# Three edits to the order of the loads: weight sums one pair later, early activations behind the last weights with two more raw buffers, fetches from the fourth block on

## The chip, the core and the metric

The kernel runs on one core of one Trainium2 chip. The metric is the device time in microseconds of one execution. Before the change it is 1907.91 us, the median of three runs (1906.57 to 1908.58). PE is TensorE, DVE is VectorE, ACT is ScalarE, POOL is GpSimd, and SP is SyncE, which here only issues DMAs.

## The reference, cut to what matters

One decoder layer on 512 tokens of width 2048, in float32: sliding-window attention with sinks, then a gated MLP with a causal convolution of width 3 over the positions.

```python
h = rms_norm(x, norm_g[i, 0])
m = swa_sink_attention(h, swa_w_in[j], swa_w_out[j], swa_sinks[j], rel_bias_table)
x = x + rms_norm(m, norm_g[i, 1])
h = rms_norm(x, norm_g[i, 2])
...
u = h @ w_up                                  # 2048 x 11264
c = conv_w[0] * up[:, 0:S] + ...              # three positions
gate, val = jnp.split(c, 2, axis=-1)          # 5632 columns each
x = x + rms_norm((silu(gate) * val) @ w_down, norm_g[i, 3])   # 5632 x 2048
```

The change touches only the MLP: the end of the preparation for its up-projection `h @ w_up`, and the passage from there to the down-projection `... @ w_down`.

## The kernel before, in words

**Numbers.** Each float32 operand is split into a high and a low half: ACT writes the high half, DVE subtracts it for the low half (`split`, L63 to L65). A product is three matmuls (`prod`, L88): high by high and the two mixed ones. The halves of weights live in a ring of slots (`halves`), five of them (`wsp`) in the up-projection, each 4 KB and 4 KB per partition, and eight in the down-projection, where the other three (`wsp3`) lie where the normalized activations `ah`, `al` were.

**Up-projection.** The 5632 gate columns and 5632 value columns are cut into 44 pairs of blocks of 128 columns, `f` = 0 to 43. Pairs 0 to 3 are multiplied in the plain way, pair 3 by halves of the tokens (`up_by_tokens`), because the operands `forms[7]` and `forms[1]` are written over parts of `ah` and `al` as soon as these have been used: their sources wait in the tiles k7 and k1 (pool `tk`). Pairs 4 to 43 use Strassen's scheme in Winograd's form (`up_pair`, L691): four weight blocks of 512 KB (`bw`, six buffers), four sums of them on DVE, seven half-size products of 24 matmuls of 256 columns each, that is 168 matmuls per pair. Then `gate` (L588) does the convolution, the SiLU and the multiplication on ACT and DVE, and POOL issues the store of the result to the DRAM tensor `hd`.

**Sums of down-projection weights.** The down-projection uses the same scheme on 22 blocks (`kp`). Four sums of weights for each are made ahead of time and stored in the DRAM tensor `td`. Those of kp 0 to 5 are made before; those of kp 6 to 21 beside the up-projection, in two ways: `weight_sums` (four loads issued by SP, four additions on DVE, four stores issued by POOL) and `queue_sums` (four loads on SP, additions and stores as DMAs of POOL). Both use the four buffers `ts` of pool `tsu`, which lies on the right side of the on-chip memory, where k7 and k1 were. In the loop over pairs (`i = f - 4`) `weight_sums` starts ahead of each pair with `i % 5 == 0`, its additions lie in the pair after it, and `queue_sums` follows that pair.

**Passage to the down-projection.** After `kp` has reached 22 (in the round `i` = 36, that is pair 40) pool `tsu` is closed and a tile of 16 KB per partition is opened in its place for blocks 0 to 15 of the activations `hd[1, 0]`; four fetches of 512 KB for it are put into SP's queue there (L741, L742). The rest of that quarter (`hq10b`, blocks 16 to 21) and the other three quarters are fetched within the first three products of the down-projection, one fetch at every second weight block (L799). These tiles, and the second pair of buffers for raw weights (`wraw2`), lie in space that pools of the up-projection held: the forms, the convolution's tiles `c`, the weight blocks.

**Down-projection.** Seven products (`product`, L793), each over 22 blocks; each block is one weight load of 512 KB (`weight_form`, L781, from `td` or from the weights themselves), a split, and 12 matmuls of 512 columns. Every four blocks `act_form` makes the halves of the activations. Raw weights have four buffers: `wraw` and `wraw2`, two each, used in turn.

**What sets the order.** Matmuls (`mm`) and the SP loads that go through `in_turn` (L138) are pinned to the order of the program on their engine, so SP issues the loads, `ts`, `bw`, fetches and raw weights strictly one after another, and one that has to wait holds all behind it. The order on ACT, DVE and POOL is laid out by the planner when the kernel is built (`schedule_with_timeline_sim=True`); on the chip each engine follows its list in order.

Of the kernel before, what the change touches and what calls it, by code (L numbers as in the profile page):

```python
# [11 lines left out]
F32 = mybir.dt.float32  # L12
# [6 lines left out]
P = 128  # L19
# [16 lines left out]
NP = NF // 2  # L36
HALF = S // 2
# [4 lines left out]
def trunk(ctx, tc, xT, x, grow, table, onehot, masked, sinks, conv,  # L42
          wkv, wq, wo, wup, wdn, out):
    nc = tc.nc
    pool = lambda name, bufs, **kw: tc.tile_pool(name=name, bufs=bufs, **kw)

    const = ctx.enter_context(pool("const", 1))
    wraw = ctx.enter_context(pool("wraw", 2))
# [8 lines left out]
    def bank(i):  # L57
        return ps.tile([P, 512], F32, name=f"b{i}", bufs=1)
# [4 lines left out]
    def split(hi, lo, src):  # L63
        nc.scalar.activation(hi, src, AF.Copy)  # L64
        nc.vector.tensor_tensor(lo, src, hi.bitcast(F32), ALU.subtract)  # L65

    def halves():
        p = ring["slots"][ring["next"] % len(ring["slots"])]
        ring["next"] += 1
        return p.tile([P, 1024], F32R, name="wh"), p.tile([P, 1024], F32R, name="wl")  # L70
# [67 lines left out]
    def in_turn(o, i):  # L138
        tc.keep_in_program_order(nc.sync.dma_start(o, i))  # L139

    def weight_sums(kp, sums, paced=False):
        t = [sums.tile([P, 1024], F32, name="ts") for _ in range(4)]
        for q in (0, 2, 1, 3):
            (in_turn if paced else nc.gpsimd.dma_start)(t[q], wdn[4 * kp + q])
        yield
        for q, o in ((2, 0), (0, 1), (1, 2), (3, 1)):
            nc.vector.tensor_tensor(t[q], t[q], t[o], ALU.add)
            nc.gpsimd.dma_start(td[kp, :, q, :], t[q])
            yield

    def queue_sums(kp, sums):
        t = [sums.tile([P, 1024], F32, name="ts") for _ in range(4)]
        for q in (2, 0, 1, 3):
            in_turn(t[q], wdn[4 * kp + q])

        def add(q, o):
            nc.gpsimd.dma_start(t[q], o, accum_op=ALU.add)

        def store(q):
            nc.gpsimd.dma_start(td[kp, :, q, :], t[q])  # L160

        add(2, wdn[4 * kp])
        add(0, wdn[4 * kp + 1])
        store(2)
        add(1, t[2])
        store(0)
        add(3, t[1])
        store(1)
        store(3)

    def step(g, n=1):
        for _ in range(n):
            next(g, None)

    with ExitStack() as att:
# [10 lines left out]
        with ExitStack() as ph:  # L186
# [26 lines left out]
            for kt in range(KT):  # L213
                if kt == 0:
                    for h in range(2):
# [3 lines left out]
                        if h == 0:  # L219
                            w = halves()  # L220
                            raw = wraw.tile([P, 1024], F32, name="raw")
# [241 lines left out]
    with ExitStack() as op:  # L463
        sums = op.enter_context(pool("tso", 4))
# [5 lines left out]
        g1 = gp.tile([P, D], F32, name="g1")  # L470
# [63 lines left out]
        for b, bk in enumerate((2, 5, 6, 7)):  # L534
            o = bank(bk)
            for kt in range(KT):
# [3 lines left out]
                if b < 2:  # L540
                    if kt == 0:
                        g = weight_sums(4 + b, sums)
# [23 lines left out]
    batches = [(g, min(g + GB, NP)) for g in range(0, NP, GB)]  # L566
    hq = {}

    def fetch(m, par, g0, g1):
        t, k0 = next((t, k) for t, k, k1 in hq[m, par] if k <= g0 < k1)  # L570
        in_turn(t[:, g0 - k0:g1 - k0, :], hd[m, par, :, g0:g1, :])

    with ExitStack() as us:
# [14 lines left out]
        def gate(f, o):  # L588
            cg = conv_half(o[0], f, 0)
            nc.scalar.activation(cg, cg, AF.Silu)  # L590
            cv = conv_half(o[1], f, 1)
            nc.vector.tensor_tensor(cv, cg, cv, ALU.mult)  # L592
            kp, par = divmod(f, 2)
            nc.gpsimd.dma_start(hd[:, par, :, kp, :].rearrange("m p t -> p m t"),  # L594
                              cv.rearrange("p (m t) -> p m t", m=2))
# [71 lines left out]
        tsu = ExitStack()  # L667
        sums = tsu.enter_context(pool("tsu", 4, side="right"))

        def block(f, r, c):  # L670
            t = bw.tile([P, 1024], F32, name="bw")
            in_turn(t, wup[4 * f + 2 * c + r])
            return t

        def form(t):
            w = halves()
            split(*w, t)
            return w

        def times(o, n, w, fresh):  # L680
            o3 = o[:, :HALF].rearrange("p (a b) -> p a b", a=2)
            a = forms[n]
            for k in range(8):
                prod(o3, cols(w, k), tuple(v[:, :, k, :] for v in a), fresh and k == 0, k == 7, not fresh)

        def shot(o, name):
            t = un.tile([P, HALF], F32, name=name)
            nc.scalar.activation(t, o[:, :HALF], AF.Copy)  # L688
            return t

        def up_pair(f, g):  # L691
            X, Y, Z = (bank(k) for k in ((0, 1, 6), (3, 4, 7))[f % 2])
            ug = un.tile([P, S], F32, name="ug", bufs=2)
            uv = un.tile([P, S], F32, name="uv", bufs=2)
            b11, b21 = block(f, 0, 0), block(f, 1, 0)
            t = wraw.tile([P, 1024], F32, name="raw")
            nc.vector.tensor_tensor(t, b11, b21, ALU.add)  # L697
            times(X, 2, form(t), True)
            s1 = shot(X, "s1")
            step(g)  # L700
            b12 = block(f, 0, 1)
            times(Z, 7, form(b12), True)
            s7 = shot(Z, "s7")
            nc.vector.tensor_tensor(t, t, b12, ALU.add)
            times(X, 5, form(t), False)
            s2 = shot(X, "s2")
            step(g)
            nc.vector.tensor_tensor(b11, b11, b12, ALU.add)  # L708
            times(Z, 6, form(b11), False)
            b22 = block(f, 1, 1)  # L710
            nc.vector.tensor_tensor(t, t, b22, ALU.add)
            times(X, 3, form(t), False)
            s3 = shot(X, "s3")
            step(g)
            nc.vector.tensor_tensor(ug[:, :HALF], Z[:, :HALF], s2, ALU.subtract)
            times(Y, 1, form(b21), True)
            nc.vector.tensor_tensor(uv[:, :HALF], s3, s7, ALU.subtract)
            times(X, 4, form(b22), False)
            nc.vector.tensor_tensor(ug[:, HALF:], s1, Y[:, :HALF], ALU.subtract)
            nc.scalar.activation(uv[:, HALF:], X[:, :HALF], AF.Copy, scale=-1.0)  # L720
            gate(f, (ug, uv))

        kp = 6
        for f in range(4, NF):
            i = f - 4
            if i % 5 == 0 and kp < NP:
                work = weight_sums(kp, sums, True)
                step(work)
                kp += 1
            up_pair(f, work if i % 5 == 1 else iter(()))  # L730
            if i % 5 == 1:
                step(work)
            if i % 5 == 1 and kp < NP:
                queue_sums(kp, sums)
                kp += 1
            if kp == NP and tsu:
                tsu.close()
                tsu = None
                early = ctx.enter_context(pool("early", 1, side="right"))
                hq[1, 0] = [(early.tile([P, 16, HALF], F32, name="hq10"), 0, 16)]  # L740
                for g0, g1 in batches[:4]:  # L741
                    fetch(1, 0, g0, g1)  # L742


    acts.close()
# [3 lines left out]
    y = acc.tile([P, NT, D], F32, name="y")  # L749
    g3 = acc.tile([P, D], F32, name="g3")  # L750
    rest = ctx.enter_context(pool("rest", 1))
    hq[1, 0].append((rest.tile([P, NP - 16, HALF], F32, name="hq10b"), 16, NP))
    raws = (wraw, ctx.enter_context(pool("wraw2", 2)))
    for m, par in ((0, 1), (1, 1)):
        hq[m, par] = [(rest.tile([P, NP, HALF], F32, name=f"hq{m}{par}"), 0, NP)]
    small = ctx.enter_context(pool("small3", 4))
    last = ctx.enter_context(ExitStack())
    hq[0, 0] = [(last.enter_context(pool("hq00", 1)).tile([P, NP, HALF], F32, name="hq00"), 0, NP)]
    coming = [(1, 0, *g) for g in batches[4:]] + [(*q, *g) for q in ((0, 0), (0, 1), (1, 1)) for g in batches]
    nc.scalar.dma_start(g3, grow[2:3, :].to_broadcast([P, D]))  # L760

    XB, ZB = (3, 4, 6, 7), (0, 1, 2, 5)
# [16 lines left out]
        return hi, lo  # L779

    def weight_form(src, kp):  # L781
        raw = raws[kp % 2].tile([P, 1024], F32, name="raw")
        table, q = src
        in_turn(raw, td[kp, :, q, :] if table else wdn[4 * kp + q])
        hi, lo = halves()
        split(hi, lo, raw)
        return hi, lo
# [5 lines left out]
    def product(o, form, src, fresh, tail=0):  # L793
        kept = []
        for g0, g1 in batches:
            af = act_form(*form, g0, g1)
            for kp in range(g0, g1):
                wf = weight_form(src, kp)
                if coming and kp % 2 == 0:  # L799
                    fetch(*coming.pop(0))  # L800
                if kp >= NP - tail:
                    kept.append((kp, af, g0, wf))
                    continue
                for t in range(2):
                    for e in range(2):
                        multiply(o, kp, af, g0, wf, t, e, fresh)
        return kept
# [13 lines left out]
    sums = {}  # L821
# [23 lines left out]
    product(z_, (a11, a21, 1), (0, 1), True)  # L845
    keep(x_, 1, 0)
    product(x_, (a12, a21, 1), (1, 1), False)
    keep(z_, 0, 1)
    product(z_, (a12, a11, -1), (1, 0), False)
# [93 lines left out]
```

## Time and profile before

| what | value |
|---|---|
| median of three runs | 1907.91 us |
| the profiled execution, its own time | 1905.1 us |
| its span, first to last instruction | 1903.1 us |
| PE busy | 1859.6 us (98%), 11822 matmuls |
| DVE busy | 1456.7 us (77%) |
| ACT busy | 982.3 us (52%) |
| POOL busy | 124.0 us (7%) |
| mean granted TensorE clock | 0.988 of full speed |
| read from HBM, written | 309.29 MB, 72.39 MB (201 GB/s over the span) |

Times in a profile are microseconds from the span's start. PE's busy time comes from matmuls that overlap, so it says little; the distance between the starts of neighbouring matmuls says more. The clock of TensorE is either 2.4 GHz (1.00) or half of that (0.50). A releaser behind an arrow is the instruction or DMA whose end let the waiting instruction go. SPq is SP's list of DMA issues; an issue that shows `x4` with a length is four of them from the first to the last.

### The profile page before, as it was taken

Reading aid. Unit: us, or ns where it says so; the run is one execution under the profiler, and the core shown is the slowest. Engines: PE = TensorE matmul, PEld = TensorE weight load, DVE = VectorE, ACT = ScalarE, POOL = GpSimd, SP = SyncE. Lnnn points to the kernel's source line nnn. Section 1 sums busy time; section 2 is a strip of 40 time slices with the busy share of each in tenths; the row PEclk is TensorE's granted clock in tenths of the full one; section 3 lists DMA queues with packets and bytes.
Section 4 is the critical chain, followed back from the end, with each engine's and each line's share of the span. In section 5 each row is a group of like instructions: output and inputs, shape, how many; then the busy total and the mean of one; then the engine's idle time right before and its main releaser. Section 6 shows DMA issues by size and latency. Waiting matters only on the chain.

```text
span 1903.1 us, 30165 instructions
## 1 busy us (share of the span) xinstructions
PE 1859.6 (98%) x11822; PEld 1688.7 (89%) x11822; DVE 1456.7 (77%) x2047; ACT 982.3 (52%) x1566; POOL 124.0 (7%) x196
## 2 busy tenths in 40 slices
PE   9999999999999599999999999999998999999998
PEld 7888888888899599999999999999997888888886
DVE  5468888754787689898989898989875666666875
ACT  6357777622443355555555555555544555545553
POOL 0000000012100111101010101010100000000000
PEclk9999999999999799999999999999998999999999
DMA  9533234499641767667585758575652876575673
GB/s 306 157 98 97 93 119 144 149 348 335 245 166 61 263 190 255 210 228 232 200 249 211 244 202 266 193 242 206 200 208 90 326 275 212 176 245 187 245 249 113
DMA packets 112397, 392.02 MB, mean 206 GB/s; under 512 B 13216, under 2 KB 15488, under 8 KB 110336
## 3 DMA queue, kind: packets, MB, share of 16 engines
q1 hardware_dynamic: 83968, 293.86, 44.8%
q0 software_dynamic: 24256, 87.04, 14.4%
q10 hardware_dynamic: 4032, 9.21, 1.5%
q8 instruction: 92, 1.51, 0.3%
q14 instruction: 49, 0.40, 0.1%
HBM read 309.29 MB, written 72.39 MB: 201 GB/s over the span
## 4 chain that ended last, share of the span: by engine, by line
PE 62%; issue 2%; DMA 1%; DVE 1%; ACT 0%; POOL 0%; DVEq 0%; SPq 0%; ACTq 0%; POOLq 0%
PE b L83 62%; DMA bw<-in_wup 0%; DMA raw<-td 0%; DVE wl L65 0%; DMA hd<-c 0%; DVE x L839 0%; POOL hd L594 0%; DVE raw L697 0%; DVE bw L708 0%; ACT wh L64 0%; ACT junk L828 0%; DVE y L830 0%; DVEq L939 0%; DVE c L592 0%; SPq L139 0%
## 5 line engine op out<-in xcount | busy, mean ns | idle before, releaser
L64 ACT ACTIVATE wh<-raw 128x1024 fp32r<-128x1024 f32 (+1 forms) x371 | 388.9, 1056 | 485.0 <-PE b L83 275.8
L65 DVE TENSOR_TENSOR wl<-raw,wh 128x1024 fp32r<-128x1024 f32 (+1 forms) x371 | 449.6, 1219 | 212.0 <-ACT wh L64 210.6
L83 PE MATMUL b<-ah,wh 128*128 128x256 f32 (+1 forms) x1824 | 563.6, 309 | 18.5 <-ACT wh L64 18.5
L83 PE MATMUL b<-ah,wl 128*128 128x256 f32 (+1 forms) x1824 | 557.2, 305 | 2.6 <-DVE wl L65 2.6
L83 PE MATMUL b<-al,wh 128*128 128x256 f32 (+1 forms) x1824 | 556.3, 305 | 0.4 <-DVE al L65 0.4
L83 PEld LDWEIGHTS b<-ah,wh 128*128 128x128 f32 x1824 | 351.1, 192 | 31.0 <-ACT wh L64 20.4
L83 PEld LDWEIGHTS b<-ah,wl 128*128 128x128 f32 x1824 | 350.6, 192 | 18.3 <-DVE wl L65 3.6
L83 PEld LDWEIGHTS b<-al,wh 128*128 128x128 f32 x1824 | 351.2, 193 | 10.9 <-DVE al L65 0.6
L83 PE MATMUL b<-wh 128*128 128x512 f32 x616 | 241.2, 392 | 6.8 <-ACT wh L64 6.8
L64 ACT ACTIVATE wh<-bw 128x1024 fp32r<-128x1024 f32 x160 | 169.1, 1059 | 147.8 <-PE b L83 144.1
L83 PE MATMUL b<-wl,wh 128*128 128x512 f32 x616 | 241.4, 392 | 1.7 <-DVE wl L65 1.7
L83 PE MATMUL b<-wh,wl 128*128 128x512 f32 x616 | 241.1, 391 | 0.0
L65 DVE TENSOR_TENSOR wl<-bw,wh 128x1024 fp32r<-128x1024 f32 x160 | 194.2, 1218 | 7.6 <-ACT wh L64 6.7
L83 PEld LDWEIGHTS b<-wh 128*128 128x128 f32 x616 | 116.4, 189 | 32.2 <-ACT wh L64 7.8
L83 PEld LDWEIGHTS b<-wl,wh 128*128 128x128 f32 x616 | 116.5, 189 | 26.7 <-DVE wl L65 2.6
L83 PEld LDWEIGHTS b<-wh,wl 128*128 128x128 f32 x616 | 116.5, 189 | 24.1
L83 PE MATMUL b<-wh,ah 128*128 128x512 f32 x320 | 126.5, 395 | 0.0
L83 PE MATMUL b<-wh,al 128*128 128x512 f32 x320 | 124.8, 390 | 0.0
L83 PE MATMUL b<-wl,ah 128*128 128x512 f32 x320 | 124.6, 389 | 0.0
L83 PE MATMUL b<-f6h,wh 128*128 128x256 f32 x320 | 91.4, 286 | 2.6 <-ACT s L688 2.6
L83 PE MATMUL b<-f6l,wh 128*128 128x256 f32 x320 | 91.3, 285 | 0.0
L83 PE MATMUL b<-f6h,wl 128*128 128x256 f32 x320 | 91.2, 285 | 0.0
(165 smaller groups left out, 3031.8 us busy)
## 6 DMA issues: line engine op xcount, KB each, us to landing
bw<-in_wup SPq DMA_DIRECT2D x160, 512.0 KB, 4.4
td<-ts POOLq DMA_DIRECT2D x88, 512.0 KB, 5.4
raw<-td SPq DMA_DIRECT2D x88, 512.0 KB, 5.0
raw<-in_wdn SPq DMA_DIRECT2D x66, 512.0 KB, 4.5
ts<-in_wdn SPq DMA_DIRECT2D x64, 512.0 KB, 6.2
ts<-in_wdn POOLq DMA_DIRECT2D x40, 512.0 KB, 8.4
raw<-in_wq SPq DMA_DIRECT2D x32, 512.0 KB, 3.5
raw<-in_wo SPq DMA_DIRECT2D x32, 512.0 KB, 5.0
```

Source lines behind the costliest of these rows:

```text
L64: nc.scalar.activation(hi, src, AF.Copy)
L65: nc.vector.tensor_tensor(lo, src, hi.bitcast(F32), ALU.subtract)
L83: tc.keep_in_program_order(nc.tensor.matmul(o, l, r, start=start, stop=stop, skip_group_check=more))
```

## The change

The additions for kp 6 move from pair 5 to pair 6 and their loads from ahead of pair 4 to ahead of pair 5; `queue_sums(7)` moves from behind pair 5 to behind pair 6; all later ones stay. `tsu` is closed behind the loop. Its 16 KB now hold 8 KB for blocks 0 to 7 of `hd[1, 0]` and the two buffers `wraw2`; only two fetches are issued early, behind the last weight block of the up-projection. `hq10b` grows to blocks 8 to 21. Raw weights of the down-projection go through `wraw`, `wraw`, `wraw2`, `wraw2` in turn, counted over all products. The first four fetches of the down-projection stand behind the raw loads number 3 to 6 (counted from 0), the later ones behind every second block.

```diff
@@ the loop over pairs
-            if i % 5 == 0 and kp < NP:
+            if (i == 1 or i and i % 5 == 0) and kp < NP:
                 work = weight_sums(kp, sums, True)
                 step(work)
                 kp += 1
-            up_pair(f, work if i % 5 == 1 else iter(()))
-            if i % 5 == 1:
+            adding = i == 2 or i > 5 and i % 5 == 1
+            up_pair(f, work if adding else iter(()))
+            if adding:
                 step(work)
-            if i % 5 == 1 and kp < NP:
-                queue_sums(kp, sums)
-                kp += 1
-            if kp == NP and tsu:
-                tsu.close()
-                tsu = None
-                early = ctx.enter_context(pool("early", 1, side="right"))
-                hq[1, 0] = [(early.tile([P, 16, HALF], F32, name="hq10"), 0, 16)]
-                for g0, g1 in batches[:4]:
-                    fetch(1, 0, g0, g1)
+                if kp < NP:
+                    queue_sums(kp, sums)
+                    kp += 1
+        assert kp == NP
+        tsu.close()
+        early = ctx.enter_context(pool("early", 1, side="right"))
+        hq[1, 0] = [(early.tile([P, 8, HALF], F32, name="hq10"), 0, 8)]
+        wraw2 = ctx.enter_context(pool("wraw2", 2, side="right"))
+        for g0, g1 in batches[:2]:
+            fetch(1, 0, g0, g1)
@@ the tiles of the down-projection
-    hq[1, 0].append((rest.tile([P, NP - 16, HALF], F32, name="hq10b"), 16, NP))
-    raws = (wraw, ctx.enter_context(pool("wraw2", 2)))
+    hq[1, 0].append((rest.tile([P, NP - 8, HALF], F32, name="hq10b"), 8, NP))
+    raws = {"pools": (wraw, wraw, wraw2, wraw2), "next": 0}
...
-    coming = [(1, 0, *g) for g in batches[4:]] + [(*q, *g) for q in ((0, 0), (0, 1), (1, 1)) for g in batches]
+    coming = [(1, 0, *g) for g in batches[2:]] + [(*q, *g) for q in ((0, 0), (0, 1), (1, 1)) for g in batches]
@@ weight_form
-        raw = raws[kp % 2].tile([P, 1024], F32, name="raw")
+        raw = raws["pools"][raws["next"] % 4].tile([P, 1024], F32, name="raw")
+        raws["next"] += 1
@@ product
                 wf = weight_form(src, kp)
-                if coming and kp % 2 == 0:
+                if 3 <= raws["next"] - 1 <= 6 or coming and kp % 2 == 0 and raws["next"] > 7:
                     fetch(*coming.pop(0))
```

## Rows read from the trace of the kernel before

**Rows 1.** Waits of PE, whole span: us in total, times, longest.
```profile
PE b L83 <- ACT wh L64: 25.3, 4, 16.4
```
**Rows 2.** Chain that ended last, in order of time: start, us, what.
```profile
655.88 730.41 PE b L83 x6072
...
1476.53 417.41 PE b L83 x1835
```
**Rows 3.** Timeline of SP's issues, 600 to 680: start, us, queue, line, operation.
```profile
626.56 1.75 SPq L139 DMA_DIRECT2D ts<-in_wdn  x4
628.36 23.44 SPq L139 DMA_DIRECT2D bw<-in_wup  x8
```
**Rows 4.** Timelines of DVE and ACT, 585 to 680 (in brackets idle time and releaser).
```profile
603.37 1.22 DVE L615 SCALAR_TENSOR_TENSOR f4l<-xf,f4h 128x1024 fp32r<-128x1024 f32 x1
...
625.31 1.22 DVE L617 TENSOR_TENSOR al<-k,ah 128x1024 fp32r<-128x1024 f32 x1 [0.21 <-ACT ah L613]
...
639.47 1.06 ACT L64 ACTIVATE wh<-raw 128x1024 fp32r<-128x1024 f32 x1 [13.62 <-DVE raw L697]
```
**Rows 5.** Timeline of PE, 620 to 661.
```profile
623.91 0.28 PE L83 MATMUL b<-ah,wl 128*128 128x256 f32 x1
640.58 0.58 PE L83 MATMUL b<-ah,wh 128*128 128x256 f32 x1 [16.39 <-ACT wh L64]
...
655.88 0.38 PE L83 MATMUL b<-f6h,wh 128*128 128x256 f32 x1 [2.62 <-ACT s L688]
...
660.36 0.28 PE L83 MATMUL b<-ah,wh 128*128 128x256 f32 x1
```
**Rows 6.** Timelines of SP and POOL, 1380 to 1412.
```profile
1383.63 2.60 SPq L139 DMA_DIRECT2D hq<-hd  x4
1386.28 21.44 SPq L139 DMA_DIRECT2D bw<-in_wup  x8
...
1409.55 0.74 POOL L594 DMA_DIRECT2D hd<-c  x1 [27.88 <-DVE c L592]
```
**Rows 7.** Timeline of PE, 1388 to 1405.
```profile
1394.63 0.28 PE L83 MATMUL b<-f4h,wl 128*128 128x256 f32 x1
1397.03 0.53 PE L83 MATMUL b<-ah,wh 128*128 128x256 f32 x1 [2.12 <-ACT wh L64]
...
1404.01 0.28 PE L83 MATMUL b<-ah,wh 128*128 128x256 f32 x1
```
**Rows 8.** Timelines of SP and POOL, 1415 to 1510.
```profile
1428.59 0.33 SPq L139 DMA_DIRECT2D raw<-td  x1
1468.25 0.33 SPq L139 DMA_DIRECT2D hq10b<-hd  x1
1468.80 0.79 SPq L139 DMA_DIRECT2D raw<-td  x2
...
1465.57 0.71 POOL L594 DMA_DIRECT2D hd<-c  x1 [16.45 <-DVE c L592]
```
**Rows 9.** Timeline of PE, 1455 to 1482.
```profile
1461.33 0.28 PE L83 MATMUL b<-f4h,wl 128*128 128x256 f32 x1
1464.58 0.50 PE L83 MATMUL b<-wh 128*128 128x512 f32 x1 [2.97 <-ACT wh L64]
...
1476.53 0.79 PE L83 MATMUL b<-wl,wh 128*128 128x512 f32 x1 [0.47 <-DVE wl L65]
...
1480.55 0.39 PE L83 MATMUL b<-wl,wh 128*128 128x512 f32 x1
```
**Rows 10.** Timeline of ACT, 1425 to 1500.
```profile
1463.48 1.04 ACT L64 ACTIVATE wh<-raw 128x1024 fp32r<-128x1024 f32 x1
1474.16 2.20 ACT L64 ACTIVATE wh<-raw 128x1024 fp32r<-128x1024 f32 x2 [9.63 <-DMA raw<-td]
...
1478.59 1.06 ACT L64 ACTIVATE wh<-raw 128x1024 fp32r<-128x1024 f32 x1 [0.25 <-DMA raw<-td]
```
**Rows 11.** Stretch of repeating pairs: us, busy by engine, PEclk, DMA share, GB/s.
```profile
700.00:1380.00 680.00, 680.00 (x5669) 680.00 (x5669) 609.10 (x671) 358.58 (x506) 79.16 (x116) 1.00 0.68 221
```

## The prediction

> **What bounds the kernel now.** I began with the waits of PE, because PE's busy share of 98% hides where it stands: the longest class is PE behind the halves that ACT writes, 25.3 us in only four waits, one of 16.4 us [rows 1]. The chain that ended last then says where to look: from 655.88 PE runs for 730.41 us without leaving the chain, and again from 1476.53 to the end [rows 2]. So three places hold all that an order of loads can win: ahead of 655.88, just behind 1386 (655.88 + 730.41), and ahead of 1476.53. Everywhere else the pace of PE is the time. In the repeating pairs 5669 matmuls take 680 us [rows 11], 0.120 us each, so a pair of 168 takes 20.2 us; in the down-projection 1835 take 417.41 us [rows 2], 0.2275 us each. I measure each stop as the start of a matmul against where it would start at this pace, which counts the waits and the slow matmuls behind them together.
>
> **Stop 1, start of pair 4.** The last plain matmul starts at 623.91, so pair 4 could start at 624.03; it starts at 640.58. After four products of 24, the fifth starts at 660.36 [rows 5]; at full pace 624.03 + 96 x 0.12 = 635.55. Lost: 24.8 us. SP's list shows why: the four loads of `ts` go out at 626.56, the weights of pair 4 only from 628.36 [rows 3]. The `ts` buffers lie where k1 lay, and k1's last reader ends at 625.31 + 1.22 = 626.53 [rows 4]. The weights' own buffers were free since 603.37 + 1.22 = 604.6, when the last temporary was read [rows 4].
>
> **Stop 2, start of pair 41.** Last matmul of pair 40 at 1394.63, next at 1397.03; the 28th of the pair starts at 1404.01 [rows 7], against 1394.75 + 27 x 0.12 = 1397.99. Lost: 6.0 us. The four early fetches go out at 1383.63, ahead of the weights of the next pairs from 1386.28 [rows 6].
>
> **Stop 3, start of the down-projection.** The last matmul of pair 43 starts at 1461.33; call T0 = 1461.45 the moment at which the down-projection could start. It starts at 1464.58, stands twice, and its 26th matmul starts at 1480.55 [rows 9]; at full pace T0 + 25 x 0.2275 = 1467.14. Lost: 13.4 us. Raw block 0 was loaded at 1428.59; block 1 stood on SP behind the fetch into `hq10b`, which went out only at 1468.25, after the store of pair 43 that POOL issued at 1465.57 [rows 8].
>
> The three stops are 44.2 us, the most that the change can win here.
>
> **Part 1: the first sums a pair later.** SP now meets the four weight blocks of pair 4 first. They can go out at 604.6. In the kernel before, six loads of this size from 626.56 were there when DVE could add, 639.47 - 1.22 = 638.2 [rows 3, 4], 11.7 us for six, so four are there by 616.3 at the latest. An addition (1.22), ACT's half (1.06) and DVE's half (1.22) [rows 4] end by 619.8, before 624.03. The whole 24.8 us goes. Late next are the weights of pair 5, because `ts` still waits for k1 until 626.5 and now stands ahead of them: again six loads, so 638.2, without the four stores of sums that POOL then issues beside them. Pair 4 runs until 624.03 + 20.2 = 644.2, and the 3.5 us of additions and halves must start by 640.7: 2.5 us to spare. The trace doesn't show this meeting; DVE and ACT follow lists, and an addition for pair 5 listed early holds back halves of pair 4. The nearest row is the stop of that kind at 655.88: 2.62 us of waiting, and then 24 matmuls in 4.48 us where 2.9 would do [rows 5], 4.2 us together. Bounds 0 and 4.2; I take 1.0, near the lower end because of the spare time. The four additions, 4.9 us of DVE, move into pair 6: DVE is busy 609.1 of 680 us with such additions in every fifth pair, and PE does not stop there [rows 11], so I cost them at nothing; DVE's free time is 70.9 / 33.7 pairs = 2.1 us in a pair, and without the lead that the five slots give it would cost 4.9 - 2.1 = 2.8 us. `queue_sums(7)` moves with them, on SP behind the weights of pair 6 and on POOL behind the same four stores as everywhere: nothing. Gain 24.8 - 1.0 = 23.8 us (20.6 to 24.8).
>
> **Part 2: fetches behind the last weights.** Two fetches leave the place where they held the weights of pair 41, two vanish from it. What SP issues at 1386.28 can go 2.6 us sooner, and sooner still by whatever the fetches waited for `ts`. I take all 6.0 us; the lower bound is 2.6, the four issues alone, if the weights' own buffers came free no sooner. In their new place they precede raw block 0, which has over 30 us to spare (1428.59 to T0).
>
> **Part 3: two more raw buffers early, fetches from block 3 on.** Raw blocks 0 to 3 now have buffers that are free before T0, and no fetch stands between them: 48 matmuls x 0.2275 = 10.9 us of work. Behind raw 3 SP meets the fetch of blocks 8 to 11 into `hq10b`. That tile still takes space of pools that close with the up-projection, so I let it go out where it did, T0 + 6.8, and raw 4 at T0 + 7.35, in the place of raw 1 before [rows 8]. Raw 1's half was started by ACT at 1474.16, T0 + 12.7 [rows 10], and the second matmul on it at 1476.53, T0 + 15.1 [rows 9]. So PE stands from 10.9 to 15.1 with one matmul between: 3.9 us. Behind such a stop matmuls run slowly for a while: at stop 2, 6.0 - (1397.03 - 1394.75) = 3.7, less some 1.0 for the second matmul's wait on DVE's half, which takes 1.22 [rows 4], leaves 2.7; here, 12 matmuls from 1476.53 take 4.02 us instead of 2.73 [rows 9], 1.3. I take 2.7, from the whole slow stretch. Left of stop 3: 6.6 us; gain 6.8 (0 to 13.4). If ACT again puts the half of block 0 behind the gate of pair 43 (1463.48 [rows 10]), PE starts at T0 + 3.1 and slowly, four blocks last until block 4 is ready, and the loss is the same 6 to 7 us. From block 4 on each block needs a fetch and a raw load; three raw loads and a half fetch lie between 1474.16 and 1478.59 [rows 10], 1.27 us per 512 KB, so 2.5 us against 2.73 of matmuls: DMA keeps up.
>
> On the arrival of raw 4 the row says 5.4 us from issue (1468.80) to ACT's start (1474.16), with one transfer of equal size just ahead [rows 8, 10]. The Trainium skill, "DMA: Bandwidth & Descriptors", section "Anatomy of one DMA - SWDGE (gpsimd) path", gives a DMA some 2.0 us beside its bytes. With two transfers of 1.27 us this makes 4.5 us, an estimate from that page; by it the loss would be 0.8 us smaller and the time 0.8 us shorter. The row here is longer than the page's sum, and the row decides.
>
> **Sum.** 23.8 + 6.0 + 6.8 = 36.6 us. The profiled execution took 1905.1 us, so 1868.5; the median of the runs lies 2.8 us above it, so 1871.3 us.
>
> **Rivals.** (a) *Clean start of the down-projection.* If only `wraw2`'s old place waited for the last store and `hq10b` does not, raw 4 comes in time: 1871.3 - 6.6 = 1864.7. Against it: it was the fetch that went out first at 1468.25, the raw loads behind it. 0.10. (b) *The wait moves to pair 5.* SP is held until 626.5 and DVE's list stands at pair 5's first addition until 638.2, with pair 4's later halves behind it: 5 to 9 us, so 1876 to 1880. For it: 2.5 us to spare is little, and the stop at 655.88 is of this kind. 0.15. (c) *The fetches wait for the last gate.* Fetches traced behind pair 43 read `hd`; if they wait for its last store, SP stands until T0 + 6.8 with two fetches and raw 0 behind: raw 0 one transfer (1.27) later than raw 1 before, second matmul at T0 + 16.4, slow stretch 2.7, loss 18.9 instead of 6.6: 1883.6. Against it: the early fetches went at 1383.63 though the store of pair 40 (last matmul at 1394.63), ahead of them in the program, went only at 1409.55 [rows 6]. 0.07. (d) *It does not do what it says.* If pair 4 was held by something else than the order of SP's list, stop 1 stays: 1871.3 + 23.8 = 1895. For it: the releaser named is ACT, behind DVE [rows 4, 5]; against it, SP's order [rows 3]. 0.04. (e) *Slower.* The lists of ACT and DVE are laid out anew, and DVE has 2.1 us free in a pair. An order that idles DVE by more makes it the bound in the 38 pairs from 6 on: from 36.6 / 38 = 0.96 us in each pair, 3.1 us of DVE idle, the kernel is slower; at 1.5 us it takes 1871.3 + 57 = 1928. For it: 90% busy; against it: the code of a pair is unchanged. 0.03.
>
> **How the numbers follow.** The forecast has 0.58, with its own range 1868 to 1875; 0.03 is left for what I don't see. The range 1863 to 1882 takes in the forecast, (a) and (b) and leaves (c), (d), (e) out. About 0.2%, 3.8 us, is what a measurement can tell from no change here: all cases but (e) lie far below it, so faster 0.95, the same 0.02, slower 0.03.
>
> **What would show it.** SP's list with `bw` four times ahead of `ts` and no PE wait over 3 us before 660; no gap near 1390; about 10.9 us of matmuls from T0, then one stop of 3 to 4 us behind a raw load, with the fetch into `hq10b` issued some 6.8 us behind T0. Wrong would be a PE wait at pair 5, a first raw load behind T0, or gaps in the repeating pairs.

## The result and the profile after

The changed kernel takes 1879.67 us, the median of four runs (1878.99 to 1880.14); the kernel before took 1907.55 us beside it. The ratio is 0.9854, with a 95% interval of 0.9836 to 0.9871: 27.9 us faster. The forecast was 1871.3 us with a range of 1863 to 1882, so the direction and the range held, and 8.4 us of the forecast gain did not come. The profiled execution took 1879.62 us (span 1877.8, mean granted clock 0.994).

The waits of PE (total, times, longest) answer to [rows 1], the chain that ended last to [rows 2].

```profile
PE b L83 <- ACT wh L64: 9.8, 2, 6.8
...
PE b L83 <- ACT s L688: 0.9, 2, 0.7
```

```profile
703.61 682.84 PE b L83 x5688
...
1446.86 421.74 PE b L83 x1847
```

Of the 25.3 us behind ACT's halves 9.8 are left, in two waits: one of 6.8 near 631 and one of 3.0 near 1445. Between 703.61 and 1386 PE runs through.

**Stop 1.** Timelines of PE, SP, DVE and ACT of the changed kernel, 585 to 640; they answer to [rows 3 to 5].

```profile
623.71 0.28 PE L83 MATMUL b<-ah,wl 128*128 128x256 f32 x1
630.79 0.58 PE L83 MATMUL b<-ah,wh 128*128 128x256 f32 x1 [6.80 <-ACT wh L64]
...
636.96 0.32 PE L83 MATMUL b<-ah,wh 128*128 128x256 f32 x1
```

```profile
604.41 1.75 SPq L139 DMA_DIRECT2D bw<-in_wup  x4
626.36 1.75 SPq L139 DMA_DIRECT2D ts<-in_wdn  x4
628.16 28.45 SPq L139 DMA_DIRECT2D bw<-in_wup  x8
```

```profile
618.99 0.75 DVE L584 SCALAR_TENSOR_TENSOR c<-b,cw,c 128x511 f32<-128x511 f32 x1 [7.04 <-ACT c L583]
...
627.82 0.69 DVE L592 TENSOR_TENSOR c<-c,c 128x512 f32<-128x512 f32 x1
628.42 1.22 DVE L697 TENSOR_TENSOR raw<-bw 128x1024 f32<-128x1024 f32 x1
```

```profile
629.68 1.06 ACT L64 ACTIVATE wh<-raw 128x1024 fp32r<-128x1024 f32 x1 [4.02 <-DVE raw L697]
```

SP does what the change wants: pair 4's four weight blocks go out at 604.41, ahead of `ts`. But DVE adds the first two (L697) only at 628.42, right behind the last step of pair 3's gate (L592), though it stood idle for 7.04 us before 618.99. (That the two blocks were there by then is shown by a kernel further down, in which DVE adds them at 609.75.) The 25th matmul of pair 4 starts at 636.96; at full pace it would be 623.83 + 24 x 0.12 = 626.71. Lost: 10.25 us of the former 24.8. There is no second stop at pair 5.

**Stop 2.** SP, DVE and PE of the changed kernel, 1370 to 1412; [rows 6, 7] before.

```profile
1378.10 0.80 SPq L139 DMA_DIRECT2D hq<-hd  x2
1379.02 25.82 SPq L139 DMA_DIRECT2D bw<-in_wup  x6
```

```profile
1384.40 1.23 DVE L708 TENSOR_TENSOR bw<-bw 128x1024 f32<-128x1024 f32 x1 [2.42 <-DMA bw<-in_wup]
```

```profile
1390.02 0.39 PE L83 MATMUL b<-f6h,wh 128*128 128x256 f32 x1 [0.71 <-ACT s L688]
```

One wait of 0.71 us is left, some 0.9 us in all, of 6.0. It is not gone because the two fetches do not stand behind the last weight block: six loads for pairs 42 and 43 come after them. DVE waits 2.42 us for one of these, and what is queued behind it there reaches PE through ACT.

**Stop 3.** POOL, SP and ACT, then PE, around the start of the down-projection; [rows 8 to 10] before.

```profile
1446.08 0.71 POOL L594 DMA_DIRECT2D hd<-c  x1 [17.24 <-DVE c L592]
```

```profile
1448.93 0.32 SPq L139 DMA_DIRECT2D hq10b<-hd  x1
1449.35 0.38 SPq L139 DMA_DIRECT2D raw<-td  x1
```

```profile
1443.46 0.63 ACT L590 ACTIVATE c<-c 128x512 f32<-128x512 f32 x1 [0.17 <-DVE c L585]
1444.00 3.88 ACT L64 ACTIVATE wh<-raw 128x1024 fp32r<-128x1024 f32 x4
1454.56 1.06 ACT L64 ACTIVATE wh<-raw 128x1024 fp32r<-128x1024 f32 x1 [6.68 <-DMA raw<-td]
```

```profile
1441.84 0.28 PE L83 MATMUL b<-f4h,wl 128*128 128x256 f32 x1
1445.09 0.50 PE L83 MATMUL b<-wh 128*128 128x512 f32 x1 [2.98 <-ACT wh L64]
1446.86 0.80 PE L83 MATMUL b<-wl,wh 128*128 128x512 f32 x1 [1.27 <-DVE wl L65]
...
1453.39 0.39 PE L83 MATMUL b<-wh,wl 128*128 128x512 f32 x1
```

T0 is now 1441.96. All four raw blocks are there, but ACT makes their halves (L64 x4) only behind the last gate (L590). The 18th matmul starts at 1453.39; full pace gives T0 + 17 x 0.2275 = 1445.83. Lost: 7.56 us of 13.4. Raw block 4, whose half ACT could start only at 1454.56, then stops nothing.

The three gains are 24.8 - 10.25 = 14.55, 6.0 - 0.9 = 5.1 and 13.4 - 7.56 = 5.85, together 25.5 us; the profiled executions differ by 1905.1 - 1879.62 = 25.5. The medians differ by 27.9, because the profiled execution before lay 2.5 us below the median of 1907.55 and the one after lies at its median. A figure of one execution is good to about 1 us: the same start of the down-projection, which five of the runs below leave as it is, loses 6.1 to 6.9 us in their traces and 7.56 here; the stretch of slow matmuls behind the waits differs in length.

### The profile page after: what moved, and what is told of

It reads as the page before. It is cut to its first block, busy times and chain, and to the rows that moved or that the text cites. A ratio compares the mean times of both kernels' runs of the same rounds, so it can differ in the third digit from the quotient of the medians.

```text
span 1877.8 us, 30181 instructions
## 1 busy us (share of the span) xinstructions
PE 1853.6 (99%) x11822; PEld 1684.3 (90%) x11822; DVE 1455.2 (77%) x2047; ACT 980.7 (52%) x1566; POOL 123.8 (7%) x196
## 4 chain that ended last, share of the span: by engine, by line
PE 95%; DVE 2%; DMA 1%; issue 1%; ACT 1%; SPq 0%; DVEq 0%; ACTq 0%
PE b L83 94%; PE b L86 2%; DMA bw<-in_wup 1%; DVE wl L65 0%; DMA raw<-in_wkv 0%; ACT wh L64 0%; DVE c L585 0%; DVE raw L697 0%; DVE bw L708 0%; DVE raw L711 0%; DVE c L584 0%; DVE x L841 0%; DVE x L625 0%; ACT ah L613 0%; ACT s L688 0%
## 5 line engine op out<-in xcount | busy, mean ns | idle before, releaser
L64 ACT ACTIVATE wh<-raw 128x1024 fp32r<-128x1024 f32 (+1 forms) x371 | 388.3, 1055 | 458.3 <-PE b L83 269.6
L83 PEld LDWEIGHTS b<-ah,wl 128*128 128x128 f32 x1824 | 349.6, 192 | 16.6 <-DVE wl L65 2.0
L64 ACT ACTIVATE wh<-bw 128x1024 fp32r<-128x1024 f32 x160 | 168.9, 1058 | 138.9 <-PE b L83 137.6
L83 PE MATMUL b<-f5h,wh 128*128 128x256 f32 x320 | 90.6, 283 | 0.0
L83 PE MATMUL b<-f5l,wh 128*128 128x256 f32 x320 | 90.6, 283 | 0.0
```

The costliest lines, as they stand in the source:

```text
L83: tc.keep_in_program_order(nc.tensor.matmul(o, l, r, start=start, stop=stop, skip_group_check=more))
```

## The experiments

My theory after the result: SP's order is right, and what is left of stop 1 and of stop 3 is the place of ready work on the lists of DVE and ACT, behind the gate of pair 3 and of pair 43. In the built program, as I read it, the first SP load behind the opening of a pool hangs on that opening and not on the load ahead of it; no trace shows that by itself. `tsu` is opened ahead of pair 4 and waits for k1's last reader. So, as I read it, the planner took pair 4's loads for late and put its first addition last; and the early fetches, the first behind the opening of `wraw2`, were free to move ahead of weight loads. The rival: pair 4 is held by slots, data or banks, which no list can mend.

**The parts alone.** The first run is the kernel before with the first part of the change, the second is the changed kernel without it:

```diff
-            if (i == 1 or i and i % 5 == 0) and kp < NP:
+            if i % 5 == 0 and kp < NP:
...
-            adding = i == 2 or i > 5 and i % 5 == 1
+            adding = i % 5 == 1
```

> Only the first part of the change: the kernel before with the sums of the seventh block one pair later (part sums traced in the second pair of the loop, additions in the third). Theory A (the three parts of the change act apart, and what is left of the stop at the start of pair 4 comes from the order of the engines' lists alone): the stop at the start of pair 4 loses about 10 us instead of 24.8, so 14.5 us less than the kernel before, about 1893 us. Theory B (the other two parts work back on the pairs, by raw buffers or by the place of the fetches): more or less than 12 to 17 us. Theory C (the sums' place did nothing, the shorter stop comes from elsewhere): 1907.

> The changed kernel with the sums' schedule of the kernel before: early fetches behind the last pair, two more raw buffers and fetches from the fourth weight block on are kept. Theory A (the parts act apart): the stop at the start of pair 4 is back at its 24.8 us, the gains of 5.1 us at pair 41 and 5.9 us at the start of the down-projection stay: 11 us less than the kernel before, about 1896 us. Theory B (the parts share a gain): the time is over 1 us from 1896, and with the run of the first part alone the two gains don't add up to the 27.9 us of the whole change.

Measured: 1892.26 us (ratio 0.9924, 0.9908 to 0.9941) and 1892.72 (0.9928, 0.9913 to 0.9943), with 1906.33 for the kernel before beside them. That is 14.1 and 13.6 us, together 27.7 of the 27.9 of the whole: the parts act apart. The first has the changed kernel's wait at pair 4 (6.80 us, at 631.04). The second gave 2.6 us more than the 11 I had, which is over the 1 us that theory A allowed, though the two gains do add up. Its trace loses 24.2 us at stop 1 (waits of 18.18, 1.82 and 1.67 us), 1.1 at stop 2 and 6.4 at stop 3, against 24.8, 6.0 and 13.4 before: 12.5 us, and its profiled execution won as much (1905.1 to 1892.62). So some 1.5 of the 2.6 us are smaller losses at stops 1 and 3; the rest comes from the kernel before, whose profiled execution lay below the median of 1906.33.

**What holds pair 4.** Two ways to the same order of lists. The first only opens the pool later:

```diff
-        held.close()
-        tsu = ExitStack()
-        sums = tsu.enter_context(pool("tsu", 4, side="right"))
...
             i = f - 4
+            if i == 1:
+                held.close()
+                tsu = ExitStack()
+                sums = tsu.enter_context(pool("tsu", 4, side="right"))
```

The second leaves the pool and writes pair 4's first four split blocks ahead of pair 3's last settling (cut to what matters; the comments are added here):

```diff
+                if m:
+                    pre = lead()      # pair 4's loads, additions and halves
+                    pin[0] = True     # settling and gate of pair 3 held behind
                 for c in range(2):
                     k = slice(4 * c, 4 * c + 4)
                     settle(n, kept[n][:, :, k, :], k, (-1.0, 1.0)[m])
```

> The changed kernel, with the opening of the pool for the sums (and the release of the first-block buffers that it takes the place of) moved from ahead of pair 4 to the second turn of the pairs' loop. Nothing that is computed or loaded changes; pair 4's first weight loads now follow the loads ahead of them in the program's order, and not the opening of the pool. Theory A (pair 4's first addition stood behind the gate of pair 3 on VectorE's list, because the planner took pair 4's weights for late): the addition moves ahead of the gate, the stop at the start of pair 4 shrinks from 10.3 us to 0 to 2, the time from 1879.7 to about 1870.5 (1869 to 1872). Theory B (pair 4 is held by something that the list only shows: its slots, its weights or ScalarE's work): 1879.7 as before, within 1 us. Theory C (the addition ahead of the gate holds up pair 3's settling, whose banks pair 4 or 5 waits for): a stop of 3 us or more at pair 4 or 5 in its place, 1873 to 1880.

> The changed kernel, with the pool for the sums where it was, but the first four split weight blocks of pair 4 (their additions and halves) written ahead of the last settling of pair 3, and that settling and gate held behind them in the engines' lists. A second way to the same order. Theory A (the order of VectorE's and ScalarE's lists around pair 3's gate is what is left of the stop): 0 to 2 us of the 10.3 remain, about 1870.5 us (1869 to 1872), as with the pool opened later. Theory B (held by something else): 1879.7. Theory C (settling late now holds pair 4 or 5 by its banks): a new stop of 3 us or more, 1873 to 1880; it then shows here and may be absent with the pool opened later.

Measured: 1873.53 us (0.9832, 0.9817 to 0.9846) and 1874.78 (0.9835, 0.9820 to 0.9849). DVE, SP and PE of the kernel with the pool opened later:

```profile
609.75 1.23 DVE L693 TENSOR_TENSOR raw<-bw 128x1024 f32<-128x1024 f32 x1 [4.79 <-DMA bw<-in_wup]
...
649.21 1.23 DVE L693 TENSOR_TENSOR raw<-bw 128x1024 f32<-128x1024 f32 x1 [1.60 <-DMA bw<-in_wup]
```

```profile
604.39 1.75 SPq L139 DMA_DIRECT2D bw<-in_wup  x4
627.51 1.75 SPq L139 DMA_DIRECT2D ts<-in_wdn  x4
629.31 25.07 SPq L139 DMA_DIRECT2D bw<-in_wup  x8
```

```profile
652.95 0.58 PE L83 MATMUL b<-f5h,wl 128*128 128x256 f32 x1 [2.83 <-DVE wl L65]
```

SP's loads go out at the same time as in the changed kernel, and the first addition (L693 here) moves from 628.42 to 609.75. PE does not wait at pair 4 at all: the order of the list was the cause, and slots, data and banks had room for it. Theory C's number came with another mechanism: the stop went to pair 5. Pair 6's first addition waits 1.60 us for a load that SP issued behind the four `ts`, with pair 5's halves behind it on DVE; PE stands 2.83 us, and 12 slow matmuls follow. The second way stops PE at the same place; DVE and PE of that kernel:

```profile
648.81 1.22 DVE L723 TENSOR_TENSOR raw<-bw 128x1024 f32<-128x1024 f32 x1
```

```profile
652.54 0.38 PE L83 MATMUL b<-f5h,wl 128*128 128x256 f32 x1 [2.00 <-DVE wl L65]
```

Here DVE works without a gap from 639.21 to 656.49, so no load holds it, and pair 6's first addition (L723) again stands ahead of pair 5's half. The place on the list is common to both ways; the late load is shown only for the first.

**The second stop.** Pool and sums another pair later, so that pair 5's loads, too, stand ahead of `ts`, and then the second batch of sums a pair later too (against the kernel with the pool opened later; the matching change of `adding` is left out):

```diff
-            if i == 1:
+            if i == 2:
                 held.close()
...
-            if (i == 1 or i and i % 5 == 0) and kp < NP:
+            if (i == 2 or i and i % 5 == 0) and kp < NP:              # first run
+            if (i in (2, 6) or i >= 10 and i % 5 == 0) and kp < NP:   # second run
```

> The changed kernel with the pool for the sums opened in the third turn of the pairs' loop and the seventh block's sums there too: part sums in pair 6, additions in pair 7 (one pair later than the change has them), so that pair 5's weight loads, too, go out ahead of the four table loads. In the run with the pool opened one turn earlier pair 4 ran without a stop, and PE then stood 2.83 us at pair 5 (at 652.95 us of the span), where VectorE's first addition waited for a weight load that was issued behind the four table loads at 627.5. Theory A (the queue behind the table loads makes that second stop): PE does not wait at pair 4 nor at pair 5, all 10.3 us of the stop are gone, 1869.5 us (1868 to 1871.5). Theory B (as many transfers in as little time: the stop only moves on to pair 6 or 7): PE stands there 2 to 3 us, 1873 to 1875, no better than the pool opened one turn earlier (1873.5).

> The kernel with the sums from the third turn on, with the second batch of sums also one pair later (turns 2, 6, 10, 15 and so on, and not 2, 5, 10, 15). With batches at turns 2 and 5 pair 4 and pair 5 ran without a stop, and PE stood 1.81 us at 712.7 of the span, where VectorE waited for the second batch's table loads (their buffers came free only with the first batch's stores), then ran slow until 717.7: some 3.5 us. Theory A (the batches stood too close): that wait goes too, 3.5 us less than that kernel, 1869.6 us (1868 to 1871). Theory B (four batches' transfers and the weights fill the DMA whatever the distance): a wait of 1.5 us or more at some later pair, 1872 to 1874.

Measured: 1873.15 us (0.9822, 0.9807 to 0.9837) for the first, no better than the run before it. No wait at pairs 4 and 5, but one at pair 8; PE, SP and DVE of this kernel, and its chain ahead of the wait:

```profile
712.73 0.39 PE L83 MATMUL b<-f5h,wh 128*128 128x256 f32 x1 [1.81 <-ACT s L684]
```

```profile
688.65 12.39 SPq L139 DMA_DIRECT2D ts<-in_wdn  x4
```

```profile
704.57 1.23 DVE L147 TENSOR_TENSOR ts<-ts 128x1024 f32<-128x1024 f32 x1 [3.58 <-DMA ts<-in_wdn]
```

```profile
688.91 8.24 DMA ts<-ts
697.55 3.15 DMA td<-ts
```

So theory B, though at pair 8 and not at pair 6 or 7, with a price of 3.5 us (1.81 of waiting, then 17 matmuls at 0.208 us): the next batch's four loads take 12.39 us to go out, because their buffers are free only after the additions and stores that POOL's queue does on the batch before (the two rows of the chain), and an addition waits for them on DVE. The chain goes on through a weight load that SP issued behind them (702.08 to 710.41), so both may count. With the batches four pairs apart this goes as well: 1869.83 us (0.9802, 0.9788 to 0.9815), expected 1869.6, and from 602 to 760 PE keeps 0.120 us without a gap (us, busy by engine, granted clock, DMA share, GB/s):

```profile
602.00:760.00 158.00, 158.00 (x1317) 157.92 (x1317) 140.23 (x153) 81.47 (x111) 17.77 (x26) 1.00 0.70 234
```

All 10.25 us of stop 1 are recovered.

**The early fetches.** Held behind the last weight load:

```diff
+        with tc.issue_after(load[0].ins):     # the last load of block()
             for g0, g1 in batches[:2]:
                 fetch(1, 0, g0, g1)
```

> The changed kernel with the two early fetches held behind the last weight load in SyncE's order, as the change meant them. In the changed kernel they stand ahead of the last six weight loads, and the loads of pairs 42 and 43 wait behind them. Theory A (that is the cause of the 0.7 us wait at 1390): this wait goes, 0.5 to 1 us less, so 1879 with no difference that 3 rounds show. Theory B (the fetches then come too late for the first activations of the down-projection): its start loses 2 us or more beyond the 7.6 us of the changed kernel, 1881 to 1884.

Measured: 1879.35 us (0.9855, 0.9840 to 0.9870). The fetches now go out at 1405.30, behind the weights, and no wait of PE is left between 1360 and 1440. Theory A; its 0.7 us is below what these runs can show, and this trace has a wait of 0.82 us at 705.07, where the changed kernel's has one of 0.23 at 703.61.

**The start of the down-projection.** Pools opened within the last pair, the first halves written ahead of its gate; then the same with fetches from the sixth block on; and that last step alone in the changed kernel (cut to what matters; the comments are added here):

```diff
             times(X, 4, form(b22), False)
+            if start:
+                start()         # pools, fetches, first activation and raw halves 0 to 2
+                pin[0] = True   # the gate's ACT and DVE work held behind
...
-                if 3 <= raws["next"] - 1 <= 6 or coming and kp % 2 == 0 and raws["next"] > 7:
+                if 5 <= raws["next"] - 1 <= 8 or coming and kp % 2 == 0 and raws["next"] > 9:
```

> The changed kernel with the opening of the pools for the early activations and the two more raw buffers moved into the last pair: the early fetches behind the last weight load, the first activations' halves and those of the first three raw weight blocks written ahead of the last gate, the gate's ScalarE and VectorE work held behind them. Fetches go on from the fourth block on, as in the change. Theory A (the first halves stand behind the last gate in the lists, and that alone makes the first matmuls of the down-projection late): no wait at its start; with blocks 0 to 2 early PE comes to block 3 sooner and now stands there, since its load goes out behind a fetch that waits for the last store: 3.9 to 6.6 us lost instead of 7.6, so 1 to 3.7 us less than the changed kernel, 1876 to 1878.7. Theory B (the first matmuls wait for data or a bank, not for the list): 1879.7. Theory C (the gate is now late, and the store and all fetches behind it): over 7.6 us lost, 1881 or more.

> The same kernel as the run with the forms ahead of the gate, with the fetches from the sixth block on and not from the fourth. Theory A (once the first blocks are early, the fetch that stands ahead of raw block 4 is what stops PE): no wait of over 1 us in the first 60 us of the down-projection, the 7.6 us of the changed kernel's start go to 0 to 1.5, 1872 to 1873.5. Theory B (raw block 4 is late for another reason, as its buffer or the DMA queue): a wait of 3 us or more stays there, 1876 to 1879.

> The changed kernel with nothing but the fetches moved from the fourth to the sixth block on. With the first halves ahead of the gate this same move took the stop at raw block 4 away (1880.8 to 1874.7 us). Theory A (the two limits of the start stand in a row: as long as the first halves come behind the last gate, raw block 4 is early enough and its order is worth nothing): no difference, 1879 to 1880, and a wait of 2.9 to 3.0 us at the first matmul of the down-projection as before. Theory B (the fetches' place costs by itself, whatever the start does): 4 to 6 us less, 1874 to 1875.5.

Measured: 1880.76 us (0.9863, 0.9848 to 0.9878), 1874.66 (0.9830, 0.9813 to 0.9846) and 1879.27 (0.9852, 0.9839 to 0.9866). PE and SP of the first of these:

```profile
1442.46 0.50 PE L83 MATMUL b<-wh 128*128 128x512 f32 x1 [0.47 <-ACT uv L757]
...
1458.13 0.80 PE L83 MATMUL b<-wh 128*128 128x512 f32 x1 [4.48 <-ACT wh L64]
```

```profile
1451.43 0.32 SPq L139 DMA_DIRECT2D hq10b<-hd  x1
1451.85 0.38 SPq L139 DMA_DIRECT2D raw<-td  x1
```

PE starts 0.6 us behind T0 (1441.83 here) instead of 3.1, and then stands at raw block 4. Theory A was right on the mechanism and wrong on the price: the gate, now held behind the halves, sends its store later (POOL issues it at T0 + 6.8 and not T0 + 4.1), the fetch into `hq10b` goes out at T0 + 9.6 and not 7.0, and the loss is some 9 us. That part is theory C.

With the fetches later, only short waits are left; PE of that kernel:

```profile
1443.27 0.50 PE L83 MATMUL b<-wh 128*128 128x512 f32 x1 [0.47 <-ACT uv L757]
...
1464.15 0.50 PE L83 MATMUL b<-wl,wh 128*128 128x512 f32 x1 [0.58 <-DVE wl L65]
```

This is 5.0 us below the changed kernel. No wait is over 1 us, as theory A had it, but the time is 1.2 us above its range of 1872 to 1873.5; the executions go from 1871.96 to 1877.45. The same move of the fetches alone is worth nothing:

```profile
1445.77 0.49 PE L83 MATMUL b<-wh 128*128 128x512 f32 x1 [2.97 <-ACT wh L64]
```

PE waits for ACT's half as before, although ACT can start on raw block 4 at T0 + 9.6 and not T0 + 12.6. Two limits stand in a row, and taking away either one alone gave nothing; both together gave 5.

**All together.** The pool and sums of the run at 1869.83 with the start of the run at 1874.66:

> All that the runs point to together: the pool for the sums opened in the third turn, sums at turns 2, 6, 10, 15 and so on, the early fetches behind the last weight load, the first halves of the down-projection ahead of the last gate, fetches from the sixth block on. Theory A (the stops at both ends add up: 10.3 us at pairs 4 to 9 and some 5.5 of the 7.6 us at the start of the down-projection): 16 us less than the changed kernel, 1863.5 us (1862 to 1866). Theory B (what the one end gives is lost at the other or in between, as an engine's list that is laid out anew): 1869 or more.

Measured over five rounds: 1863.07 us (1862.26 to 1865.17), ratio 0.9771 (0.9758 to 0.9784), as theory A had it (1863.5). That is 44.0 us below the kernel before (1907.08 beside it) and 16.6 below the changed one. All waits of PE in this kernel:

```profile
PE b L83 <- DVE zero L190: 1.5, 1, 1.5
PE b L83 <- DVE wl L65: 0.8, 1, 0.8
PE b L83 <- ACT uv L753: 0.5, 1, 0.5
PE b L83 <- DVE al L65: 0.4, 1, 0.4
```

## Why the prediction was right, and which step failed

**The three stops** were the right places. Their sum, 44.2 us, was named as the most that the change can win. It was counted on profiled executions, and by these the last run wins 42.8 (1905.1 to 1862.26; 44.0 by the medians).

**Luck in the range.** The forecast's own range, 1868 to 1875, was missed. The time lies in the part of 1863 to 1882 that was there for rival (b), 1876 to 1880, and the mechanism of (b) did not occur: there the wide range held by luck. The sum also added 2.8 us to come from the profiled execution to the median; after the change the two agree (1879.62 and 1879.67), so the median missed its forecast by only 8.4 us, the profiled execution by 11.1. Of the signs named ahead, SP's list and the time of the fetch into `hq10b` came. The sign "no PE wait over 3 us before 660" did not: there is one of 6.80. Nor did the one stop behind raw block 4.

**Stop 1: the failed step.** "An addition, ACT's half and DVE's half end by 619.8, before 624.03. The whole 24.8 us goes." The first two loads came as forecast (by 616.3 at the latest; in the run with the pool opened later DVE could add at 609.75), but the addition ended at 629.64. I had taken the time at which data is there for the time at which DVE uses it. The prediction itself says that DVE follows a list and that it is laid out anew, and uses that only for pair 5 and for rival (e). What was left of the stop is 10.25 us instead of 1.0: 9.25 of the 11.1 us by which the profiled execution missed 1868.5.

**Rival (b), the wait moves to pair 5,** did not occur in the changed kernel, I think because pair 4 came 7 us late and gave pair 5's loads that time. Once pair 4 was on time, the mechanism was there in the run with the pool opened later: SP held until 627.5 by `ts`, weights behind it, an addition listed early. It cost 4.4 us in all (2.99 and 0.26 in two gaps, 12 matmuls x 0.092), just above the upper bound of 4.2 and below the rival's 5 to 9. The second way to the same order lost 5.3 us there, with a second wait of 0.94 us at 660.75. My 2.5 us to spare were not there.

**Stop 2:** gain 5.1 for 6.0. That the fetches would stand behind the last weights was wrong, and so, in this place, the kernel did not do what the diff says; it cost 0.9 us.

**Stop 3:** 7.56 us left for 6.6, by the variant that the text gave ("If ACT again puts the half of block 0 behind the gate", PE at T0 + 3.1) and not by the main one. Both are limits of this start, as the three runs on it show; the larger hid the other. Rival (a) is excluded by `hq10b` at T0 + 6.97, (c) by the fetches at 1378.10. The time from issue of raw block 4 to ACT's start, forecast as 5.4 us, is 5.2 (1449.35 to 1454.56), again with a transfer just ahead. The Trainium skill, "DMA: Bandwidth & Descriptors", section "Anatomy of one DMA - SWDGE (gpsimd) path", by its 2.0 us beside the bytes, gave 4.5 as an estimate; this run, too, is longer than that. That section of the Trainium skill is on DMAs that POOL issues, and SP issued this one.

**Rival (d)** holds for 10.25 of the 24.8 us: with SP's order changed, that part was held by DVE's list. **Rival (e)** is excluded: in the repeating pairs 5585 matmuls take 670 us, 0.120 us each as in [rows 11]. The stretch in the changed kernel (us, busy by engine, granted clock, DMA share, GB/s):

```profile
710.00:1380.00 670.00, 670.00 (x5585) 670.00 (x5585) 598.88 (x659) 351.96 (x498) 78.72 (x116) 1.00 0.69 224
```

**What stays open:** that the planner placed the addition late because of the pool's opening is read from the program and from two runs that changed the list; its reckoning itself was not measured. Open, too, is what puts DVE's list in the way at pair 5 in the second way, where no load is late.

## What to carry to other kernels

When a load is moved earlier, follow its data through every list to the engine that bounds the kernel: the first consumer must stand early on its own list too, or the load only waits in the buffer. Look for what else pins or frees an instruction, such as the opening of a pool between a load and the one before it. And where two waits lie in a row, the value of removing one shows only with the other gone, so try them together before calling either worthless.

## What the runs showed of the hardware

What a wait of PE costs beyond itself varies. Stretches of the changed kernel, then of the one with the pool opened later, then of the one with the sums from the third turn on, in the same columns; the third figure from the end is the granted clock:

```profile
630.79:636.96 6.17, 5.66 (x25) 5.37 (x26) 6.17 (x7) 2.90 (x3) 0.55 (x1) 0.50 0.98 379
1390.02:1393.00 2.98, 2.98 (x25) 2.98 (x25) 2.88 (x4) 1.17 (x2) 0.74 (x1) 1.00 0.56 176
```

```profile
652.95:655.87 2.92, 2.92 (x14) 2.92 (x14) 2.92 (x4) 0.00 (x0) 0.72 (x1) 0.51 0.26 56
```

```profile
712.73:714.14 1.41, 1.41 (x11) 1.41 (x12) 1.41 (x3) 1.16 (x2) 0.34 (x1) 1.00 0.96 317
714.14:717.68 3.54, 3.54 (x19) 3.54 (x18) 3.54 (x5) 0.77 (x1) 0.00 (x0) 0.52 0.43 175
```

Behind the waits of 6.80 and 2.83 us PE runs at half clock (the 1.2 GHz level) at once, for 6.2 and 2.9 us; behind the one of 0.71 us it does not fall. Behind the one of 1.81 us it first runs 1.4 us at full clock, and only then 3.5 us at half, while it is busy. So the 0.71 us wait cost 0.9 us, and the 1.81 us wait 3.5. Six more waits of 0.72 to 1.19 us, in the runs with the pool opened later, pair 4's blocks written early, the fetches pinned and the fetches later, are followed by matmuls at 0.12 us from the second one on. At the start of the down-projection the same two waits of 2.97 or 2.98 and 1.27 us were followed by 13 matmuls of 0.42 us and more in the changed kernel, and by 6 in the run with the pool opened later, where 0.23 us is full pace.
